# Depthwise convolution: all products from ScalarE, summed by GpSimd in SBUF instead of by TensorE in PSUM

## The chip, the cores and the metric

The kernel runs on one core of one Trainium2 chip. Its time is the device time of one execution in microseconds (us), and the figure of a version is the median of three executions. A core has five engines that work side by side, each through its own queue in a fixed order: TensorE (PE, with its weight loads as PEld), VectorE (DVE), ScalarE (ACT), GpSimd (POOL) and SyncE (SP), which issues the DMAs. An instruction that waits for a semaphore holds up everything behind it on its engine. TensorE writes to PSUM alone, the other memory on the core is SBUF.

## The reference

Two transformer-like blocks run one after the other on 256 tokens of 1024 features, in fp32. The change lies in the second block, which has three branches: attention to a memory, a convolution, and a two-way recurrence (RWKV-7) that the kernel computes with small triangular solves. Then an output projection and a layer of 16 experts follow. Shortened:

```python
def conformer_conv(pc, conv_w, conv_b, ln_g, ln_b):
    val, gate = jnp.split(pc, 2, axis=-1)
    u = val * jax.nn.sigmoid(gate)                      # 256 tokens x 384 channels
    u = lax.conv_general_dilated(u, conv_w[:, None, :], window_strides=(1,),
        padding=[(15, 15)], dimension_numbers=('NWC', 'WIO', 'NWC'),
        feature_group_count=384) + conv_b               # 31 taps, each channel by itself
    return silu(layer_norm(u, ln_g, ln_b))              # over the channels
def second_block(...):
    o_att, o_conv = memory_cross_attention(...), conformer_conv(...)
    o_rwkv = rwkv7_bidirectional(...)
    x = x + jnp.concatenate([o_att, o_conv, o_rwkv], axis=-1) @ w_out
    x = x + expert_choice_ffn(rms_norm(x), ...)         # 16 experts
```

## The kernel before

Activations lie with features on the 128 partitions and the 256 tokens along them. The 384 channels of the convolution are three tiles of 128, `u[:, 0]`, `u[:, 1]` and `u[:, 2]`, each 286 wide (256 tokens and 15 zeros on each side). A tap is one product of a shifted view `u[:, i, t:t+256]` with one number for each partition. VectorE computes tiles 0 and 1 (`conv`, L1493): one `scalar_tensor_tensor` for each tap multiplies and adds into `cacc[:, i]`, 60 of them and 2 first products. Tile 2 goes another way (`conv_pe`, L1483): ScalarE multiplies into a tile `cp`, TensorE multiplies `cp` with the unit matrix, and its 31 products add up in one PSUM bank, `pconv`, from which ScalarE writes `cacc[:, 2]`. `conv` goes on with the layer norm over the three tiles: sums over partitions by matmuls with ones (`pm`), square root, scale, SiLU, and the split into two parts (`oc`) that the output projection reads.

The convolution is woven with the recurrence. Its direction d needs, for each of three pairs of heads: `scores` (L1544: matmuls `psab`, then VectorE masks them into `LM`), `diagonal` (L1561: VectorE takes the 16x16 blocks out, tile `tm` and sums `N`; GpSimd adds the unit matrix to `LM`), and `values` (L1571: matmuls `pkt`, `prh`, `py0`, which ScalarE copies out as `bt`, `rh`, `ysum`). `blocks16` (L1608) then solves the 16x16 blocks in 15 steps: a matmul `prep`, and on VectorE a product `g` and an addition into `Gc`. `prep` needs `N` alone, so it can run ahead as far as PSUM banks are free; `g` and `Gc` are a chain. At its end VectorE spreads the blocks (`Gm`), TensorE transposes them (`pt`, L1636), and `levels` (L1645) joins blocks to 32, 64 and 128 with matmuls `pp` and `pg`. `finish` (L1684) uses the result.

What comes when is set by the generators and by the table `W` (L25): `weave` (L1751) takes one step of a main generator, and so many of the others after it. First `first_scores(0)` runs with `conv_pe`, then `other_scores(0)` and `first_scores(1)` with `blocks16(0)`, `conv_pe` and `conv`, then `levels(0)` with `blocks16(1)`, `conv` and `conv_pe`. A scheduler of the framework then puts the instructions of each engine in an order of its own, with semaphores where one needs another; that order is fixed when the kernel is built. Tiles of one tag take turns in a fixed number of buffers (`bufs`), and whoever writes a buffer again waits for its last readers. PSUM has 8 banks: five with tag `ps` (among them `pkt`, `prh`, `py0`, `prep` and half of `psab`), three with tag `pw`.

Weights of the experts (1 MB pieces, tile `ew`) are loaded into a ring of buffers that grows as tiles of the recurrence become free; SP issues them in order, and each waits until its buffer is free.

Of the kernel before, what the change touches and what calls it, by code (L numbers as in the profile page):

```python
# [11 lines left out]
F32 = mybir.dt.float32  # L12
F32R = mybir.dt.float32r
U32 = mybir.dt.uint32
AF = mybir.ActivationFunctionType
ALU = mybir.AluOpType
# [5 lines left out]
DECAY = 0.606531  # L22
MASKED = -1e30
LEAD = 5
W = 2, 2, 2, 2, 1, 0, 2, 1, 1, 8  # L25
OPB = 5, 5, 5, 5, 0
E1 = 4, 3, 2, 1
PRE = 0
# [227 lines left out]
class Body:  # L256
# [960 lines left out]
    def branches(self, x2, hi, lo, ob):  # L1217
# [53 lines left out]
        u = rb.tile([128, 3, 286], F32, name="u")  # L1271
# [188 lines left out]
        for j in range(2):  # L1460
            ps = self.pst("pvt")
# [18 lines left out]
        cw = self.v("conv_w_2").rearrange("p (k i) -> p k i", k=31)  # L1480
        cacc = rb.tile([128, 3, 256], F32, name="cacc")

        def conv_pe():  # L1483

            ps = self.pst("pconv")
            for t in range(31):
                p_ = wk2.tile([128, 256], F32, name="cp", tag="cp", bufs=2)
                self.act(p_, u[:, 2, t:t + 256], AF.Copy, scale=cw[:, t, 2:3])
                self.mm(ps[:, 0:256], self.ident, p_, t == 0, t == 30)
                yield  # L1490
            self.act(cacc[:, 2], ps[:, 0:256], AF.Identity, bias=self.v("conv_b_2", 2))

        def conv():  # L1493
            for i in range(2):
                self.ts(cacc[:, i], u[:, i, 0:256], cw[:, 0, i:i + 1], ALU.mult, self.v("conv_b_2", i), ALU.add)
                for t in range(1, 31):
                    self.stt(cacc[:, i], u[:, i, t:t + 256], cw[:, t, i:i + 1], cacc[:, i], ALU.mult, ALU.add)
                    yield
            ps = self.pst("pm")
            for i in range(3):  # L1500
                self.mm(ps[:, 0:256], self.ones, cacc[:, i], i == 0, i == 2)
            self.stt(cacc, ps[:, None, 0:256].to_broadcast([128, 3, 256]), -1.0 / 384, cacc, ALU.mult, ALU.add)
            yield
            sq = aa[0]
            self.act(sq, cacc, AF.Square)
            yield
            ps = self.pst("pm")
            for i in range(3):
                self.mm(ps[:, 0:256], self.ones, sq[:, i], i == 0, i == 2)
            rn = sq[:, 0]  # L1510
            self.act(rn, ps[:, 0:256], AF.Sqrt, scale=1.0 / 384, bias=self.eps[:, 1:2])
            nc.vector.reciprocal(rn, rn)
            yield
            self.tt(cacc, cacc, rn[:, None, :].to_broadcast([128, 3, 256]), ALU.mult)
            for i in range(3):
                self.ts(cacc[:, i], cacc[:, i], self.v("conv_ln_g_2", i), ALU.mult, self.v("conv_ln_b_2", i), ALU.add)
            yield
            s = aa[0]
            self.act(s, cacc, AF.Sigmoid)
            self.tt(cacc, cacc, s, ALU.mult)  # L1520
            yield
            ob.extend(self.kv.tile([128, 2, 256], F32R, tag=n, name="oc", bufs=1) for n in ("km", "vm"))
            ob.append(self.sq.tile([128, 2, 256], F32R, tag="sq", name="oc", bufs=2))
            for i in range(3):
                self.put_split(ob[2 + i][:, 0], ob[2 + i][:, 1], cacc[:, i])
            self.dbg("oc", cacc)
# [67 lines left out]
        def first_scores(d):  # L1594

            for i in range(3):
                scores(d, i, 0)
                yield
                diagonal(d, i)

        def other_scores(d):
            for i in range(3):
                scores(d, i, 1)
                yield
                values(d, i)
                yield
# [131 lines left out]
        def bonus():  # L1738
            for i in range(3):
                bn = wk3.tile([128, 256], F32, name="bn", tag="bn", bufs=1)  # L1740
                self.stt(bn, kds[:, i], self.v("r_k_2", i), r[:, i], ALU.mult, ALU.mult)
                ps = self.pst("pm")
                self.mm(ps[:, 0:256], self.bo, bn, True, True)
                self.tt(vv[:, i], vv[:, i], ps[:, 0:256], ALU.mult)
                self.stt(vv[:, i], vv[:, i], self.v("lnx_b_2", i), gate[:, i], ALU.add, ALU.mult)
                self.act(gate[:, i], gate[:, i], AF.Copy, scale=self.v("lnx_g_2", i))
                yield

        ct = conv()

        def weave(main, *others):  # L1751
            for _ in main:
                for g, n in others:
                    for _ in range(n):
                        next(g, 0)

        def chain(*gens):
            for g in gens:
                yield from g
        cpe, late, bon, f0 = conv_pe(), other_scores(1), bonus(), finish(0)  # L1760
        weave(first_scores(0), (cpe, W[0]))
        b0, b1 = blocks16(0), blocks16(1)
        weave(chain(other_scores(0), first_scores(1)), (b0, 2), (cpe, W[1]), (ct, W[2]))
        self.go(b0)
        weave(levels(0), (b1, 1), (ct, W[3]), (cpe, W[4]), (late, W[5]))
        self.go(b1)
        self.go(cpe)
        lv = levels(1)
        weave(itertools.islice(lv, W[9]), (ct, W[6]), (f0, 1), (late, W[7]), (bon, W[8]))
        for g in (late, bon, ct, f0):  # L1770
# [38 lines left out]
        pool, tag = late[1]  # L1809
# [382 lines left out]
```

## Time and profile before

| | us |
|---|---|
| three executions | 1173.88, 1176.94, 1177.71 (median 1176.94) |
| the profiled execution | 1175.34 |
| its span, from the first to the last instruction | 1173.5 |
| busy in the span: PE / DVE / ACT / POOL | 1062.8 / 508.2 / 417.8 / 44.4 |

The profile is one execution. Times in it count from the start of the span. A matmul in fp32 shows as two records. Lines such as L299 or L284 are those of helpers through which all matmuls or all `tensor_tensor` go, so groups are told apart by the names of the tiles: `pconv<-cp,cm` writes `pconv` and reads `cp` and `cm` (which holds the unit matrix). A busy TensorE is not one at its peak: the ends of matmuls are modelled. Recorded durations of instructions that follow each other on VectorE or ScalarE overlap by some 0.06 to 0.09 us.

### The profile page before, as it was taken

To read this page: it belongs to the slowest core of one execution; us is meant where nothing else is said; L and a number is where in the kernel's file an instruction comes from. 1 tells how busy PE (TensorE), PEld (TensorE's weight loads), DVE (VectorE), ACT (ScalarE), POOL (GpSimd) and SP (SyncE) were. 2 spreads that over 40 slices of the span, in tenths; PEclk is the share of its full clock that TensorE was granted. 3 is DMA by queue.
4 is the path that set the end of the run, shared out by engine and by line. 5 is a ranking of instruction groups with operands and counts; after the bars stand their busy time and mean duration, and the time that the engine had idled before them with its cause. 6 is when DMAs were issued, how large, how long until landed. Compare 5 with 4: busy or idle time off the path is not lost.

```text
span 1173.5 us, 19272 instructions
## 1 busy us (share of the span) xinstructions
PE 1062.8 (91%) x8188; PEld 755.2 (64%) x8188; DVE 508.2 (43%) x964; ACT 417.8 (36%) x718; POOL 44.4 (4%) x50
## 2 busy tenths in 40 slices
PE   5999999999999999999999998989978877788785
PEld 4886676899999999898679886434422222222222
DVE  3544356586555555659888546212111111111102
ACT  4542467656444444576434534101100000000003
POOL 0000000021000000101210002000000000000000
PEclk9999999999999999999799998999997888877877
DMA  9974545455655553420401378999999999999996
GB/s 354 364 278 167 179 169 208 176 182 182 209 180 181 185 190 120 166 109 1 180 1 46 144 300 337 385 419 419 420 418 420 419 419 419 419 420 419 420 419 254
DMA packets 46918, 313.88 MB, mean 267 GB/s; under 512 B 6128, under 2 KB 6896, under 8 KB 10480
## 3 DMA queue, kind: packets, MB, share of 16 engines
q1 hardware_dynamic: 46832, 312.66, 67.7%
q8 instruction: 64, 1.05, 0.4%
q14 instruction: 22, 0.18, 0.0%
HBM read 311.59 MB, written 1.05 MB: 266 GB/s over the span
## 4 chain that ended last, share of the span: by engine, by line
PE 65%; DMA 25%; DVE 4%; ACT 4%; issue 1%; POOL 1%; SPq 0%; ACTq 0%; POOLq 0%; DVEq 0%
PE pw L299 22%; PE acc L299 9%; DMA ew<-in_w_e_down_dram 9%; DMA ew<-in_w_e_up_dram 9%; DMA ew<-in_w_e_gate_dram 7%; PE pd L299 5%; PE pgu L299 4%; PE psab L299 2%; PE pada L299 2%; PE pv L299 2%; PE pqf L299 2%; PE pconv L299 1%; PE pg L299 1%; PE pp L299 1%; PE py L299 1%; PE prep L299 1%
## 5 line engine op out<-in xcount | busy, mean ns | idle before, releaser
L284 DVE TENSOR_TENSOR split<-raw,split 128x1024 fp32r<-128x1024 f32 (+2 forms) x148 | 176.8, 1203 | 114.6 <-ACT split L278 114.1
L299 PE MATMUL pgu<-ew,XE 128*32 128x256 f32 x2048 | 152.9, 435 | 48.4 <-DMA ew<-in_w_e_up_dram 41.4
L278 ACT ACTIVATE split<-raw 128x1024 fp32r<-128x1024 f32 (+2 forms) x148 | 151.8, 1032 | 124.5 <-PE pw L299 65.9
L299 PE MATMUL pd<-ew,hidT 128*32 128x512 f32 (+2 forms) x560 | 152.9, 601 | 8.3 <-DVE hidT L2086 7.8
L299 PEld LDWEIGHTS pgu<-ew,XE 128*32 128x32 f32 x2048 | 65.0, 120 | 127.8 <-DMA ew<-in_w_e_up_dram 68.3
L299 PEld LDWEIGHTS pd<-ew,hidT 128*32 128x32 f32 x560 | 41.7, 118 | 109.3 <-issue 94.6
L299 PE MATMUL acc<-uh,split 128*128 128x256 f32 x512 | 94.7, 283 | 0.0
L299 PE MATMUL pw<-h2h,split 128*128 128x256 f32 x512 | 92.9, 280 | 0.0
L296 DVE SCALAR_TENSOR_TENSOR hid<-pgu,rs,hid 128x256 f32<-128x256 f32 x16 | 7.7, 484 | 188.6 <-ACT hid L275 188.6
L296 DVE SCALAR_TENSOR_TENSOR ye<-pd,ig,ye 128x512 fp32r<-128x512 f32 (+2 forms) x35 | 24.6, 705 | 143.4 <-ACT ye L275 141.8
L275 ACT ACTIVATE hid<-pgu,rs 128x256 f32<-128x256 f32 x16 | 7.6, 473 | 214.0 <-PE pgu L299 214.0
L275 ACT ACTIVATE ye<-pd,ig 128x512 fp32r<-128x512 f32 (+2 forms) x35 | 22.8, 651 | 165.7 <-PE pd L299 165.7
L299 PEld LDWEIGHTS acc<-uh,split 128*128 128x128 f32 x512 | 80.8, 192 | 0.0
L299 PEld LDWEIGHTS pw<-h2h,split 128*128 128x128 f32 x512 | 79.3, 188 | 0.0
L299 PE MATMUL acc<-ul,split 128*128 128x256 f32 x256 | 72.5, 283 | 0.0
L299 PE MATMUL pw<-h2l,split 128*128 128x256 f32 x256 | 71.4, 279 | 0.0
L299 PE MATMUL pw<-hxh,split 128*128 128x256 f32 x320 | 61.7, 286 | 0.1
L299 PE MATMUL pw<-hmh,split 128*128 128x256 f32 x320 | 61.0, 288 | 0.0
L299 PEld LDWEIGHTS pw<-hxh,split 128*128 128x128 f32 x320 | 50.0, 188 | 9.5 <-issue 8.1
L299 PEld LDWEIGHTS pw<-hmh,split 128*128 128x128 f32 x320 | 50.5, 191 | 1.6 <-PE pz L299 0.5
L299 PEld LDWEIGHTS acc<-ul,split 128*128 128x128 f32 x256 | 49.0, 191 | 0.2 <-DVE ul L284 0.2
L299 PEld LDWEIGHTS pw<-h2l,split 128*128 128x128 f32 x256 | 48.0, 187 | 0.0
(441 smaller groups left out, 1741.6 us busy)
## 6 DMA issues: line engine op xcount, KB each, us to landing
ew<-in_w_e_gate_dram SPq DMA_DIRECT2D x64, 1024.0 KB, 19.9
ew<-in_w_e_up_dram SPq DMA_DIRECT2D x64, 1024.0 KB, 19.9
ew<-in_w_e_down_dram SPq DMA_DIRECT2D x63, 1024.0 KB, 19.9
raw<-in_w_mlp_dram SPq DMA_DIRECT2D x32, 1024.0 KB, 4.8
raw<-in_w_ada_dram SPq DMA_DIRECT2D x24, 1024.0 KB, 5.9
raw<-in_w_in_dram SPq DMA_DIRECT2D x18, 1024.0 KB, 5.0
raw<-in_w_branch_gate_dram SPq DMA_DIRECT2D x8, 1024.0 KB, 4.9
raw<-in_w_out_dram SPq DMA_DIRECT2D x4, 1024.0 KB, 6.9
```

Source lines behind the costliest of these rows:

```text
L275: self.nc.scalar.activation(out, in_, func, **kw)
L278: self.nc.scalar.activation(out, in_, AF.Copy)
L284: self.nc.vector.tensor_tensor(out=out, in0=a, in1=b, op=op)
L296: self.nc.vector.scalar_tensor_tensor(out=out, in0=a, scalar=s, in1=b, op0=op0, op1=op1)
L299: self.nc.tensor.matmul(out, lhsT, rhs, start=start, stop=stop, **kw)
```

## The change

ScalarE still computes all 31 products of tile 2, and now also the products of taps 16 to 30 of tile 1 (`TAPS = 16`). GpSimd adds them up in SBUF: those of tile 2 in `cacc[:, 2]`, those of tile 1 in a new tile `half` (named `chalf`). The first product of each is written there by ScalarE with the bias, so 30 + 14 additions remain. `pconv` and its 31 matmuls are gone. VectorE computes the 31 taps of tile 0 and 16 of tile 1, and adds `half` once. `cp` has three buffers instead of two. `conv` runs `conv_pool` to its end before it goes on. The first two numbers of `W` are now 3 and 4.

```diff
@@ -22,7 +22,8 @@
 DECAY = 0.606531
 MASKED = -1e30
 LEAD = 5
-W = 2, 2, 2, 2, 1, 0, 2, 1, 1, 8
+TAPS = 16
+W = 3, 4, 2, 2, 1, 0, 2, 1, 1, 8
 OPB = 5, 5, 5, 5, 0
 E1 = 4, 3, 2, 1
 PRE = 0
@@ -1480,22 +1481,32 @@
         cw = self.v("conv_w_2").rearrange("p (k i) -> p k i", k=31)
         cacc = rb.tile([128, 3, 256], F32, name="cacc")
 
-        def conv_pe():
-
-            ps = self.pst("pconv")
-            for t in range(31):
-                p_ = wk2.tile([128, 256], F32, name="cp", tag="cp", bufs=2)
-                self.act(p_, u[:, 2, t:t + 256], AF.Copy, scale=cw[:, t, 2:3])
-                self.mm(ps[:, 0:256], self.ident, p_, t == 0, t == 30)
-                yield
-            self.act(cacc[:, 2], ps[:, 0:256], AF.Identity, bias=self.v("conv_b_2", 2))
+        half = wk2.tile([128, 256], F32, name="chalf")
+
+        def conv_pool():
+
+            for i, ts, o in ((2, range(31), cacc[:, 2]), (1, range(TAPS, 31), half)):
+                for t in ts:
+                    x = u[:, i, t:t + 256]
+                    if t == ts[0]:
+                        self.act(o, x, AF.Identity, scale=cw[:, t, i:i + 1], bias=self.v("conv_b_2", i))
+                    else:
+                        p_ = wk2.tile([128, 256], F32, name="cp", tag="cp", bufs=3)
+                        self.act(p_, x, AF.Copy, scale=cw[:, t, i:i + 1])
+                        self.tp(o, o, p_, ALU.add)
+                    yield
 
         def conv():
-            for i in range(2):
-                self.ts(cacc[:, i], u[:, i, 0:256], cw[:, 0, i:i + 1], ALU.mult, self.v("conv_b_2", i), ALU.add)
-                for t in range(1, 31):
+            for i, n in ((0, 31), (1, TAPS)):
+                if i:
+                    self.ts(cacc[:, 1], u[:, 1, 0:256], cw[:, 0, 1:2], ALU.mult)
+                else:
+                    self.ts(cacc[:, 0], u[:, 0, 0:256], cw[:, 0, 0:1], ALU.mult, self.v("conv_b_2", 0), ALU.add)
+                for t in range(1, n):
                     self.stt(cacc[:, i], u[:, i, t:t + 256], cw[:, t, i:i + 1], cacc[:, i], ALU.mult, ALU.add)
                     yield
+            self.go(cpool)
+            self.tt(cacc[:, 1], cacc[:, 1], half, ALU.add)
             ps = self.pst("pm")
             for i in range(3):
                 self.mm(ps[:, 0:256], self.ones, cacc[:, i], i == 0, i == 2)
@@ -1746,6 +1757,7 @@
                 self.act(gate[:, i], gate[:, i], AF.Copy, scale=self.v("lnx_g_2", i))
                 yield
 
+        cpool = conv_pool()
         ct = conv()
 
         def weave(main, *others):
@@ -1757,14 +1769,13 @@
         def chain(*gens):
             for g in gens:
                 yield from g
-        cpe, late, bon, f0 = conv_pe(), other_scores(1), bonus(), finish(0)
-        weave(first_scores(0), (cpe, W[0]))
+        late, bon, f0 = other_scores(1), bonus(), finish(0)
+        weave(first_scores(0), (cpool, W[0]))
         b0, b1 = blocks16(0), blocks16(1)
-        weave(chain(other_scores(0), first_scores(1)), (b0, 2), (cpe, W[1]), (ct, W[2]))
+        weave(chain(other_scores(0), first_scores(1)), (b0, 2), (cpool, W[1]), (ct, W[2]))
         self.go(b0)
-        weave(levels(0), (b1, 1), (ct, W[3]), (cpe, W[4]), (late, W[5]))
+        weave(levels(0), (b1, 1), (ct, W[3]), (cpool, W[4]), (late, W[5]))
         self.go(b1)
-        self.go(cpe)
         lv = levels(1)
         weave(itertools.islice(lv, W[9]), (ct, W[6]), (f0, 1), (late, W[7]), (bon, W[8]))
         for g in (late, bon, ct, f0):
```

The orders below are those of the built programs, one row for instructions that follow each other and read alike. First ScalarE, before: from the first product `cp` of tile 2 to the first copies (`bt`, `rh`, `ysum`) of `values` in direction 0.

```order
L275 ACTIVATE cp<-u,vec 128x256 x2
L278 ACTIVATE om<-pom 128x256
L275 ACTIVATE vv<-pad_4841,mu_4820 128x256 x2
L275 ACTIVATE cp<-u,vec 128x256 x2
L278 ACTIVATE vtok<-pvt 128x384 x2
L275 ACTIVATE cp<-u,vec 128x256 x13
L278 ACTIVATE bt_5760<-pkt 128x256
L278 ACTIVATE rh_5761<-prh 128x256
L278 ACTIVATE ysum<-py_5870 128x256
L275 ACTIVATE cp<-u,vec 128x256
```

The same stretch of ScalarE after the change:

```order
L276 ACTIVATE cp<-u,vec 128x256 x3
L279 ACTIVATE om<-pom 128x256
L276 ACTIVATE vv<-pad_4841,mu_4820 128x256 x2
L276 ACTIVATE cp<-u,vec 128x256 x6
L276 ACTIVATE chalf<-u,vec 128x256
L276 ACTIVATE cp<-u,vec 128x256 x3
L279 ACTIVATE vtok<-pvt 128x384 x2
L276 ACTIVATE cp<-u,vec 128x256 x29
L279 ACTIVATE bt_5761<-pkt 128x256
L276 ACTIVATE cp<-u,vec 128x256
L279 ACTIVATE rh_5762<-prh 128x256
L276 ACTIVATE cp<-u,vec 128x256
```

Before, 17 of 31 products stand ahead of the first `bt`; now 41 of 44 do, and the two first products (`chalf` here, `cacc` much earlier) as well. Every product from the fourth on waits until GpSimd is through with the third one before it, since `cp` has three buffers.

GpSimd before, from the last work of the projections to the first `diagonal`:

```order
L287 TENSOR_TENSOR ex_5047<-pr,ex_5047 128x3x256
L287 TENSOR_TENSOR ex_5048<-pr,ex_5048 128x3x256
L1443 COPY kds<-LM_5581 128x768
L287 TENSOR_TENSOR LM_5663<-LM_5663,pr 128x768
L1445 TENSOR_TENSOR kds<-kds,LM_5663 128x768
L1568 TENSOR_TENSOR LM_5767<-LM_5767,cm 128x512
```

GpSimd after, from its first addition of the convolution on:

```order
L288 TENSOR_TENSOR cacc<-cacc,cp 128x256
L1444 COPY kds<-LM_5581 128x768
L288 TENSOR_TENSOR cacc<-cacc,cp 128x256 x5
L288 TENSOR_TENSOR LM_5663<-LM_5663,pr 128x768
L288 TENSOR_TENSOR cacc<-cacc,cp 128x256
L1446 TENSOR_TENSOR kds<-kds,LM_5663 128x768
L288 TENSOR_TENSOR cacc<-cacc,cp 128x256 x14
L1579 TENSOR_TENSOR LM_5768<-LM_5768,cm 128x512
L288 TENSOR_TENSOR cacc<-cacc,cp 128x256 x7
L1579 TENSOR_TENSOR LM_5769<-LM_5769,cm 128x512
L288 TENSOR_TENSOR cacc<-cacc,cp 128x256 x2
L288 TENSOR_TENSOR chalf<-chalf,cp 128x256 x4
```

After the last of these rows come `LM_5770`, then the ten other additions into `chalf`, then the three `diagonal` additions of direction 1. So 34 additions stand ahead of the third `LM`, and 38 ahead of what the 41st product needs.

TensorE before, around the first `values` (with the semaphores that are waited for):

```order
L299 MATMUL pconv<-cp,cm 128x256 [waits Activation_49] x2
L299 MATMUL psab<-ex_5047 128x256
L299 MATMUL pconv<-cp,cm 128x256 [waits Activation_49]
L299 MATMUL prep<-N,sel 128x192 [waits DMAHW3_49,DVE_49]
L299 MATMUL prep<-N,sel 128x192 [waits PE_49]
L303 MATMUL pkt<-cm,aa_5045 128x128 [waits PE_49]
L303 MATMUL pkt<-cm,ex_5047 128x128
L299 MATMUL prh<-vtok,LM_5835 128x64 [waits PE_49]
L299 MATMUL prh<-vtok,LM_5835 128x64 x3
L299 MATMUL py_5870<-LM_5835,vtok 64x128 [waits DVE_49]
L299 MATMUL py_5870<-LM_5835,vtok 64x128 x3
L299 MATMUL prep<-N,sel 128x192 [waits Activation_49] x2
```

TensorE after, in the same place:

```order
L300 MATMUL prep<-N,sel 128x192 [waits DMAHW3_49,DVE_49]
L300 MATMUL prep<-N,sel 128x192
L304 MATMUL pkt<-cm,aa_5045 128x128
L304 MATMUL pkt<-cm,ex_5047 128x128
L300 MATMUL prh<-vtok,LM_5842 128x64 x4
L300 MATMUL py_5883<-LM_5842,vtok 64x128 x4
L300 MATMUL prep<-N,sel 128x192 [waits DVE_49]
L300 MATMUL prep<-N,sel 128x192 [waits Activation_49]
L300 MATMUL psab<-ex_5047 128x256 [waits Activation_49]
L300 MATMUL psab<-ex_5047 128x256
```

`pkt` is followed by `prh`, `py`, and the third and fourth `prep`; the fourth waits for ScalarE, and it gets the bank for which the copy `bt` has to be done, the `psab` behind it that of `rh`. In both versions the third or the fourth `prep` waits for ScalarE; what stands ahead of `bt` there is what moved.

## Rows read from the trace of the kernel before

**Rows 1.** which engine is busy, clock and DMA, in four stretches

```profile
core 0: us, PE busy (x) PEld busy (x) DVE busy (x) ACT busy (x) POOL busy (x), PEclk, DMA share, GB/s
554.00:558.00 4.00, 1.58 (x13) 1.20 (x12) 4.00 (x9) 0.50 (x2) 0.15 (x1) 1.00 0.00 0
558.00:571.00 13.00, 13.00 (x35) 8.64 (x36) 12.36 (x16) 3.38 (x9) 4.57 (x3) 0.51 0.97 382
...
584.00:610.30 26.30, 25.80 (x145) 18.66 (x143) 22.84 (x64) 10.03 (x23) 2.81 (x2) 1.00 0.00 1
```

**Rows 2.** the chain of waits (start us, us, what), 580 to 660

```profile
610.35 1.31 PE pt L303 x12
...
619.12 0.43 PE pconv L299 x2
...
641.94 1.30 PE pm L299 x6
...
647.45 1.30 PE pm L299 x6
```

**Rows 3.** timeline of ScalarE (start us, us, what, [idle before <-releaser])

```profile
558.04 0.91 ACT L275 ACTIVATE cp<-u,vec 128x256 f32<-128x256 f32 x2
...
584.71 0.38 ACT L278 ACTIVATE bt<-pkt 128x256 f32<-128x256 f32 x1 [0.30 <-PE pkt L303]
585.55 0.38 ACT L278 ACTIVATE rh<-prh 128x256 f32<-128x256 f32 x1 [0.46 <-PE prh L299]
```

**Rows 4.** groups of GpSimd instructions (xcount | busy us, mean ns | idle)

```profile
L1568 POOL TENSOR_TENSOR LM<-LM,cm 128x512 f32<-128x512 f32 x6 | 8.0, 1338 | 37.8 <-DVE tm L284 34.8 <-ACT cp L275 1.5 <-PE psab L299 1.4
L287 POOL TENSOR_TENSOR sa<-sa,sq 128x256 f32<-128x256 f32 x8 | 6.2, 778 | 10.1 <-ACT sq L275 9.8
...
L287 POOL TENSOR_TENSOR LM<-LM,pr 128x768 f32<-128x768 f32 x1 | 1.9, 1885 | 3.1 <-DVE LM L293 3.1
L1445 POOL TENSOR_TENSOR kds<-kds,LM 128x768 f32<-128x768 f32 x1 | 1.9, 1863 | 0.1
...
L1443 POOL COPY kds<-LM 128x768 f32<-128x768 f32 x1 | 0.8, 823 | 4.6 <-DVE LM L284 4.6
```

**Rows 5.** timeline of GpSimd, 550 to 606

```profile
550.44 3.71 POOL L287 TENSOR_TENSOR ex<-pr,ex 128x768 f32<-128x768 f32 x2 [75.96 <-DVE stm L291]
...
562.65 1.89 POOL L287 TENSOR_TENSOR LM<-LM,pr 128x768 f32<-128x768 f32 x1 [3.08 <-DVE LM L293]
...
604.97 1.55 POOL L1568 TENSOR_TENSOR LM<-LM,cm 128x512 f32<-128x512 f32 x1 [1.96 <-DVE tm L284]
```

**Rows 6.** timeline of VectorE in the same places

```profile
551.21 3.42 DVE L293 TENSOR_SCALAR LM<-aa,vec,oneka 128x256 f32<-128x256 f32 x3
...
562.39 2.42 DVE L296 SCALAR_TENSOR_TENSOR vv<-pad,vec,vv 128x256 f32<-128x256 f32 x2
...
604.91 0.48 DVE L296 SCALAR_TENSOR_TENSOR cacc<-u,vec,cacc 128x256 f32<-128x256 f32 x1
```

**Rows 7.** a group of VectorE instructions, 556.8 to 570.3

```profile
L284 DVE TENSOR_TENSOR aa<-aa,ex 128x768 f32<-128x768 f32 x2 | 1.9, 946 | 0.0
```

**Rows 8.** groups of VectorE instructions, 589.2 to 610.3

```profile
L296 DVE SCALAR_TENSOR_TENSOR cacc<-u,vec,cacc 128x256 f32<-128x256 f32 x12 | 5.7, 474 | 0.0
L284 DVE TENSOR_TENSOR LM<-psab,cr 128x512 f32<-128x512 f32 x8 | 5.5, 687 | 2.6 <-PE psab L299 2.0 <-PE py L299 0.5
...
L284 DVE TENSOR_TENSOR tm<-LM,cr 128x512 f32<-128x512 f32 x3 | 2.1, 684 | 0.0
L1566 DVE TENSOR_REDUCE N<-tm 128x64 f32<-128x512 f32 x2 | 2.0, 1015 | 0.0
```

**Rows 9.** timeline of VectorE, the fourth step of the first block solve

```profile
589.28 0.30 DVE L284 TENSOR_TENSOR g<-prep,Gc 128x144 f32<-128x144 f32 x1
```

**Rows 10.** windows of 2 us at the start of the expert stage

```profile
732.00:734.00 2.00, 2.00 (x23) 1.24 (x23) 0.25 (x2) 0.47 (x1) 0.00 (x0) 0.93 0.02 4
...
736.00:738.00 2.00, 2.00 (x25) 1.21 (x24) 0.48 (x1) 0.47 (x1) 0.00 (x0) 1.00 1.04 426
```

## The prediction

> **What bounds the kernel now.** I read the windows by stage first, then the chain of waits, then the queues of the engines that touch the convolution. In the stretch that the change rewrites (558 to about 634 us) TensorE and VectorE are both nearly full and GpSimd is nearly free: from 584 to 610.3 TensorE has records for 25.8 of 26.3 us, VectorE 22.8, GpSimd 2.8 [rows 1]. That invites the change. But the reader should look at what the stretch has to reach: the transposes `pt`, which open `levels(0)` at 610.35 [rows 2]. They need the end of the first block solve, whose chain `g`, `Gc` runs on VectorE, and that needs `prep` from TensorE, which stops as soon as the copies `bt` and `rh` on ScalarE are late, since they free its banks. Before, `bt` starts at 584.71, 0.30 after ScalarE went idle: it waits for TensorE and nothing else [rows 3]. So ScalarE's queue is not the bound now, and the question is whether it becomes one.
>
> After the stretch the delay has nowhere to go. At 732 to 734 the DMAs stand almost still (share 0.02) and from 736 they are full [rows 10]: at 732 the ring of expert weights holds all it can, and from there the DMAs follow the rate at which TensorE frees buffers. A stretch that ends x later moves all that by x.
>
> **What goes.** 31 matmuls with the unit matrix. The two late ones stand in the chain in `levels(0)`, 0.43 each [rows 2]: 0.9 us less. The other 29 lie before `pt`, where they are filling between waits; what their room is worth is in the block solve below. VectorE loses 14 steps of tile 1 and gains one addition.
>
> **What comes: 44 additions on GpSimd.** The trace has the same operation in the same shape, `sa<-sa,sq`, each waiting for the one before: 0.778 us mean [rows 4]. ScalarE needs 0.46 for a product (two in 0.91, [rows 3]), so GpSimd sets the pace and ScalarE, three buffers ahead, waits in its queue. ScalarE's order decides: 41 products stand ahead of the first `bt`, and the 41st waits for the 38th addition. GpSimd's queue up to there: 38 x 0.778 = 29.6; three `diagonal` additions of 1.338 = 4.0; the product and sum for `kds`, 1.885 + 1.863; its copy 0.823 [rows 4]. Together 38.2. The first `cp` is ready at 558.5, half of the pair at 558.04 [rows 3], so the 38th addition ends at 596.7 if nothing disturbs GpSimd.
>
> It will be disturbed. At 550.44 two GpSimd products run for 3.71, and three VectorE instructions that start at 551.21 take 3.42 instead of about 0.4 each; at 562.39 two take 2.42 instead of 0.9 beside the GpSimd product at 562.65; the other way round, the addition at 604.97 takes 1.55 against a mean of 1.338, having started 0.06 after a VectorE one of 0.48 [rows 4 to 6]. So the two take turns when both read SBUF. What a turn costs GpSimd I take as VectorE's duration less a part of each GpSimd instruction that does not grow with size: 256 more elements cost 1.338 - 0.778 = 0.56, so 0.778 - 0.56 = 0.22. The VectorE instructions in the stretch whose operands are both in SBUF, by its order, which does not change there, and one turn each: five of 768 elements at 0.946 [rows 7], twelve of 256 at 0.474 and three `tm` at 0.684 [rows 8]. That makes 5 x 0.73 + 12 x 0.25 + 3 x 0.46 = 8.0. The 38th addition ends at 604.7, the 41st product at 605.2, and `bt` starts there: 20.5 us later than the 584.71 of before. Bounds: no turns at all, 597.2; whole durations (4.7 + 5.7 + 2.1 = 12.5), 609.7.
>
> [...]
>
> **The block solve after `bt`.** When TensorE stops at the fourth `prep`, VectorE has done three steps and stands before the `g` of the fourth. Before, that `g` starts at 589.28 [rows 9] and `pt` at 610.35 [rows 2]: 21.1 us. After, it can start some 0.9 after `bt` (0.38 for the copy, one `prep`, the hand-overs), at 606.1. What VectorE has to do from there: by the order two steps of the convolution and one masking `LM` fewer (0.474 x 2 + 0.687), one `tm` and one sum `N` more (0.684 + 1.015) [rows 8]: even. So `pt` at 606.1 + 21.1 = 627.2, 16.8 later than before. Bounds: 2.6 of the 21.1 are waits for `psab` and `py` [rows 8], part of them behind `pconv`, and may go: 18 us. On the other side six additions and three of 1.338 are left to GpSimd and take turns with VectorE: 27 us.
>
> **The rest.** `conv` can go on only when GpSimd is through, some 10 us after `bt`, well before `pt`; its matmuls `pm` stand later in TensorE's order, so no wait is added there. Six of them (1.30 + 1.30, [rows 2]) move from `levels(1)` into `levels(0)`: zero, with bounds -3 and +4 for what ScalarE's table loads and the copies queued behind them do in the new place. VectorE's relief in `levels(0)` I count at nothing, because TensorE has the longer list there.
>
> TensorE's clock: 4 us with little work (1.58 busy, 554 to 558) were followed by 13 us at 0.51, the lower of its two levels [rows 1]. After the change TensorE waits some 20 us for `bt`, so it will come back at the lower level. Most of that lies beside VectorE's 21 us; I take +1, bounds 0 and 6.4 (half of those 13).
>
> **Sum** against the profiled execution: 16.8 - 0.9 + 1.0 = 16.9, so 1175.3 + 16.9 = 1192.2. Its time lies 1.6 under the median of the runs, so the forecast for a median is 1193. The bounds together give 1175.3 + 1 to 1175.3 + 36.
>
> **The rivals.**
>
> *The lock is as strict as it can be* (chance 0.16): every VectorE instruction costs GpSimd its whole length, and in the block solve VectorE in turn waits for whole additions. `bt` at 609.7, the solve 25 us: `pt` at 635.6, 25 later, 1200 to 1202. For it: the 2.42 and 3.42 [rows 6]. Against: the 3.71 [rows 5].
>
> *The late copies are hidden* (chance 0.08): `bt` at 597.2, the solve in 18 us, thus `pt` at 616.1, 5.8 later; with the 0.9 and 3 us won in `levels(1)` about 2 us remain, 1177 to 1179, no change that can be told. For it: the waits in [rows 8] and an emptier TensorE. Against: VectorE is busy nearly all through that stretch [rows 1].
>
> *It pays* (chance 0.04): TensorE's stretch shrinks by the `pconv` matmuls and nothing waits for `bt`. It would need 38 additions and the other 8.6 us of GpSimd within the 26.2 us from 558.5 to 584.7, so 0.46 us for an addition; from there on the products on ScalarE set the pace and the gain is the 0.9 and the 2.6 of waits, 1172. Against it: 0.778, eight times measured [rows 4].
>
> The forecast itself has 0.72. Its own range is 1186 to 1200.
>
> **How the numbers follow.** A measurement of this kernel tells apart changes of over 0.3%, 3.5 us. Faster by more needs "it pays" in full: 0.03. Within 0.3%: nearly all of "hidden" and the rest of "it pays", 0.08. Slower: 0.89. The range for 8 in 10 takes in the strict lock up to 1207 and, below, a `bt` halfway to its lower bound: 1183.
>
> **What would show it.** In the changed profile: GpSimd additions `cacc<-cacc,cp` back to back from 558.5, starts 0.8 to 1.1 apart; ScalarE's waits on GpSimd at its products, 10 us or more in all; the first `bt` near 605; TensorE idle or at the lower clock in the 20 us before; `pt` near 627; the ring's pause at the start of the expert stage some 17 later than 732. It is wrong if `bt` comes before 595, if the fourth `prep` doesn't wait for it, or if the stretch from `pt` to the end of `levels(1)` is shorter than before by more than 3 us.

## The result, and the profile after

The changed kernel takes 1206.72 us (median of four, 1202.7 to 1207.59), before it was 1176.95 on the same chip. The ratio is 1.0264, with a 95% interval of 1.0245 to 1.0284, so it is some 30 us slower, 31 by the ratio. The forecast was 1193, and the ratio times the 1176.94 of before lies at 1208, just over the upper end of the range. The profiled execution took 1207.59, 32.25 more than that of before. It begins 1.4 us late, long before the change (GpSimd's `ex` at 551.81 against 550.44 in [rows 5]); this is not counted below.

The windows of the same stretch, columns as in [rows 1]:

```profile
558.00:571.00 13.00, 12.57 (x37) 8.23 (x37) 12.41 (x15) 6.96 (x16) 10.70 (x10) 0.57 0.86 338
571.00:584.00 13.00, 8.79 (x25) 6.01 (x24) 13.00 (x17) 6.35 (x13) 12.14 (x13) 0.50 0.17 68
584.00:605.00 21.00, 8.54 (x30) 6.29 (x30) 8.03 (x14) 11.34 (x24) 19.59 (x26) 0.50 0.00 0
605.00:636.00 31.00, 30.53 (x87) 19.64 (x86) 14.27 (x38) 3.45 (x9) 5.24 (x6) 0.50 0.00 1
...
645.00:660.00 15.00, 15.00 (x127) 14.98 (x126) 12.62 (x38) 4.86 (x10) 0.00 (x0) 0.99 0.00 1
```

The rows from 571 and from 584 are what the prediction described: GpSimd is nearly full, and TensorE works 8.54 of the 21 us up to 605. The row from 605 to 636 is the one that it didn't have: TensorE has records for 30.53 of 31 us at clock 0.50, the lower of its two levels, and VectorE, which was to be the chain there, is busy for 14.27. Only from 645 on the clock is at the upper level again (0.99). Before, the 26 us of the same work ran at 1.00 [rows 1].

ScalarE (columns as in [rows 3]), and its group of products from 558 to 606 (xcount | busy us, mean ns | idle before, by releaser):

```profile
559.40 1.30 ACT L276 ACTIVATE cp<-u,vec 128x256 f32<-128x256 f32 x3
...
603.26 0.51 ACT L276 ACTIVATE cp<-u,vec 128x256 f32<-128x256 f32 x1 [0.29 <-POOL chalf L288]
603.68 0.36 ACT L279 ACTIVATE bt<-pkt 128x256 f32<-128x256 f32 x1
...
642.94 0.60 ACT L279 ACTIVATE Tm<-pt 128x512 f32<-128x512 f32 x1 [16.59 <-PE pt L304]
```

```profile
L276 ACT ACTIVATE cp<-u,vec 128x256 f32<-128x256 f32 x44 | 22.1, 508 | 20.9 <-POOL cacc L288 17.4 <-POOL chalf L288 3.3
```

`bt` starts at 603.68, at once behind a product that waited for GpSimd, and the products together waited 20.7 us for GpSimd's additions. Then GpSimd:

```profile
559.99 0.73 POOL L288 TENSOR_TENSOR cacc<-cacc,cp 128x256 f32<-128x256 f32 x1 [4.48 <-ACT cp L276]
...
571.73 14.17 POOL L288 TENSOR_TENSOR cacc<-cacc,cp 128x256 f32<-128x256 f32 x14
...
595.79 3.13 POOL L288 TENSOR_TENSOR chalf<-chalf,cp 128x256 f32<-128x256 f32 x4
...
600.10 7.94 POOL L288 TENSOR_TENSOR chalf<-chalf,cp 128x256 f32<-128x256 f32 x10
```

With VectorE at work 14 additions take 14.17 us, 1.01 each; while VectorE stands still (from 593.5 to 607), four take 3.13 and ten 7.94, 0.78 to 0.79 each, the 0.778 of [rows 4]. TensorE, in the same columns:

```profile
575.53 2.07 PE L300 MATMUL psab<-ex,aa 64*128 64x256 f32 x4 [3.46 <-ACT vtok L279]
...
590.99 1.01 PE L300 MATMUL prep<-N,sel 128*128 128x192 f32 x2
604.10 1.01 PE L300 MATMUL prep<-N,sel 128*128 128x192 f32 x2 [12.09 <-ACT bt L279]
...
641.79 2.82 PE L304 MATMUL pt<-cm,Gm 128*128 128x128 f32 x12 [0.24 <-DVE Gm L285]
```

The fourth `prep` waits 12.09 us for `bt`, as foreseen. Earlier, `psab` waits 3.46 us for `vtok`, a copy that also stands in ScalarE's queue behind 12 products; the prediction had missed it. `pt` starts at 641.79, 31.4 later than in [rows 2], and VectorE waits for TensorE where it had a chain to work on:

```profile
570.02 2.56 DVE L285 TENSOR_TENSOR aa<-aa,ex 128x768 f32<-128x768 f32 x1
...
607.14 0.69 DVE L285 TENSOR_TENSOR LM<-psab,cr 128x512 f32<-128x512 f32 x1 [13.68 <-PE psab L300]
...
629.54 0.69 DVE L285 TENSOR_TENSOR LM<-psab,cr 128x512 f32<-128x512 f32 x1 [4.93 <-PE psab L300]
```

The first of these rows shows the turns on VectorE's side too: the instruction of 0.946 in [rows 7] takes 2.56 beside GpSimd's `kds` and additions (before, GpSimd was idle there). At the start of the expert stage the pause of the ring lies at 764 (before at 732, [rows 10]), so what `pt` lost went to the end undiminished:

```profile
764.00:766.00 2.00, 2.00 (x23) 1.21 (x21) 0.45 (x1) 0.47 (x1) 0.00 (x0) 0.83 0.03 12
...
768.00:770.00 2.00, 2.00 (x28) 1.35 (x24) 0.48 (x1) 0.47 (x1) 0.00 (x0) 1.00 0.93 393
```

### The profile page after: what moved, and what is told of

Its sections match the earlier page's. It is cut to its first block, busy times and chain, and to the rows that moved or that the text cites. A ratio compares the mean times of both kernels' runs of the same rounds, so it can differ in the third digit from the quotient of the medians.

```text
span 1205.6 us, 19219 instructions
## 1 busy us (share of the span) xinstructions
PE 1073.1 (89%) x8126; PEld 763.1 (63%) x8126; DVE 510.2 (42%) x950; ACT 425.7 (35%) x732; POOL 81.1 (7%) x94
## 4 chain that ended last, share of the span: by engine, by line
PE 61%; DMA 26%; DVE 4%; ACT 4%; POOL 3%; issue 2%; SPq 0%; ACTq 0%; POOLq 0%; DVEq 0%
PE pw L300 21%; DMA ew<-in_w_e_up_dram 10%; PE acc L300 9%; DMA ew<-in_w_e_down_dram 8%; DMA ew<-in_w_e_gate_dram 7%; PE pd L300 4%; PE pgu L300 4%; PE pada L300 2%; POOL cacc L288 2%; PE pv L300 2%; PE pqf L300 2%; PE psab L300 2%; PE prep L300 1%; PE pg L300 1%; PE pp L300 1%
```

## The experiments

Theory A is that of the prediction, extended: `bt` comes late, TensorE stops for it, and the stop leaves TensorE at the lower clock. Theory B: the 31 products with the unit matrix had kept TensorE's clock up, and without them the block solve runs at the lower level whether `bt` is late or not. Theory C: GpSimd's additions cost the most, through their turns with VectorE, or the order of the solve does.

Times are medians of 4 to 12 executions. Ratios are to runs of before on the same chip; before took 1172 to 1177 on the chips used, so a time is held against another row's, or a forecast, by the ratio. `bt` (its first copy on ScalarE) and `pt` (its first matmul) are from the one profiled execution and count from its start; by the `ex` of [rows 5], the stretch begins 1.2 us earlier (e8) to 2.5 us later (e3) than before.

| | what | ratio [95%] | us | `bt` | `pt` | from `bt` to `pt` | clock between |
|---|---|---|---|---|---|---|---|
| before | | 1 | 1176.9 | 584.7 | 610.2 | 25.5 | 1.00 |
| after | the change | 1.0264 [1.0245, 1.0284] | 1206.7 | 603.7 | 641.8 | 38.1 | 0.50 |
| e1 | 12 products ahead of `bt` | 1.0171 [1.0148, 1.0194] | 1194.8 | 587.3 | 628.4 | 41.1 | 0.50 |
| e2 | 20 idle products before `bt` | 1.0269 [1.0243, 1.0294] | 1206.3 | 603.2 | 640.3 | 37.1 | 0.50 |
| e3 | short additions | 1.0138 [1.0111, 1.0166] | 1191.1 | 588.9 | 627.0 | 38.1 | 0.50 |
| e4 | tile 2 alone | 1.0167 [1.0138, 1.0196] | 1194.2 | 591.9 | 630.0 | 38.1 | 0.50 |
| e5 | before, short unit products | 1.0253 [1.0228, 1.0279] | 1204.2 | 596.0 | 639.3 | 43.3 | 0.50 |
| e6 | e1 with 46 idle products | 1.0154 [1.0130, 1.0177] | 1194.0 | 592.5 | 627.0 | 34.5 | mostly 1.00 |
| e7 | after with 46 idle products | 1.0245 [1.0223, 1.0267] | 1204.5 | 606.9 | 636.0 | 29.1 | 1.00 from 612 |
| e8 | before, 12 early idle products | 1.0001 [0.9984, 1.0018] | 1174.3 | 579.8 | 604.1 | 24.3 | 1.00 |
| e9 | e6 with short additions | 1.0058 [1.0037, 1.0079] | 1181.7 | 586.3 | 614.6 | 28.4 | 1.00 |
| e10 | tile 1's 15 taps on TensorE | 1.0047 [1.0028, 1.0065] | 1181.3 | 586.5 | 612.3 | 25.8 | 1.00 |
| e11 | e10 with early idle products | 1.0103 [1.0080, 1.0126] | 1187.1 | 585.2 | 614.8 | 29.5 | 1.00 |
| e12 | e2 with 28 idle products | 1.0258 [1.0229, 1.0288] | 1202.6 | 603.8 | 631.1 | 27.3 | see below |
| e13 | e3 with early idle products | 1.0066 [1.0029, 1.0104], two groups, below | 1178.2 | 589.2 | 614.8 | 25.6 | 1.00 to 610 |
| e14 | e1 with early idle products | 1.0100 [1.0070, 1.0130] | 1187.2 | 587.5 | 628.6 | 41.1 | 0.50 |

In every row, the profiled execution ends 563 to 572 us after `pt` (before 565, after the change 566). So most of the time is decided at `pt`, as the prediction had it, and what remains to be explained is `bt` and the way from `bt` to `pt`. The exceptions are e6, e7, e10 and e11, which lose another 3 to 7 us behind `pt`.

**e1, the order of ScalarE.** `in_turn` is a helper of the kernel: what is traced inside is queued behind the instruction traced before it on that engine.

```diff
-                        self.act(p_, x, AF.Copy, scale=cw[:, t, i:i + 1])
+                        with self.in_turn("Activation"):
+                            self.act(p_, x, AF.Copy, scale=cw[:, t, i:i + 1])
                         self.tp(o, o, p_, ALU.add)
```

> The changed kernel, but ScalarE issues each product behind what was traced before it, so 12 products stand ahead of the first bt instead of 41; the number of products and additions is the same. Theory A (the queue of ScalarE, and the low clock it leaves TensorE in): bt near 587, TensorE back at the upper clock by about 595, pt near 613 to 618, 1178 to 1186 us. Theory B (the products with the unit matrix were what brought TensorE's clock back): bt near 587 as well, but the clock stays at 0.50 until the transposes, pt near 623 to 630, 1189 to 1196. Theory C (the 44 additions themselves, through their turns with VectorE): 1195 or more.

`bt` came at 587.33, waiting for TensorE and not for ScalarE. Yet the clock stayed down for another 40 us, by the windows of e1:

```profile
584.00:596.00 12.00, 12.00 (x40) 8.54 (x38) 6.52 (x17) 4.88 (x11) 4.68 (x6) 0.50 0.00 1
...
608.00:620.00 12.00, 12.00 (x39) 8.40 (x39) 8.69 (x23) 5.90 (x13) 8.39 (x12) 0.50 0.01 1
...
632.00:644.00 12.00, 12.00 (x103) 11.98 (x102) 11.33 (x30) 5.39 (x11) 3.90 (x5) 1.00 0.01 1
```

That refutes theory A as the whole cause. The time, 1194.8 (1197 by the ratio), lies at the upper end of B's range and the lower end of C's and doesn't tell the two apart; the clock does speak for B.

**e2, idle products before `bt`.**

```diff
+                if d == 0 and kk == 2:
+                    for _ in range(20):
+                        with self.in_turn("PE"):
+                            self.mm(ps[:, 256:512], self.ident, u[:, 2, 0:256], True, True)
```

> The changed kernel with 20 idle products of 128x256 (unit matrix by a tile of u, result not used) on TensorE behind the third prep, where it waited 12.1 us for bt. bt stays near 603.7. Theory A: TensorE comes back at the upper clock, the stretch from bt to pt shrinks from 38.1 us to 22 to 27, 1190 to 1196. Theory C and any reason that lies in the order of the block solve: the stretch stays at 35 to 40, 1204 to 1212.

The windows of e2 around `bt` (603.2) and behind it:

```profile
596.00:600.00 4.00, 4.00 (x20) 3.54 (x19) 4.00 (x5) 1.53 (x3) 3.84 (x5) 1.00 0.00 0
...
604.00:608.00 4.00, 4.00 (x10) 2.31 (x8) 4.00 (x5) 1.69 (x5) 3.61 (x5) 0.50 0.00 0
...
612.00:636.00 24.00, 23.20 (x71) 14.98 (x70) 10.72 (x31) 1.92 (x5) 2.52 (x2) 0.50 0.00 1
```

The idle products did bring the clock up (0.81 from 592 to 596, then 1.00 and 0.97 up to 604), but it was down again one window later (0.50) and stayed there: 37.1 us from `bt` to `pt`, and no time won. It doesn't tell why, since 20 products ended 2.9 us before `bt`, and that gap could have dropped the clock; e12 closes it.

**e3, short additions.** `self.tp(o[:, 0:16], o[:, 0:16], p_[:, 0:16], ALU.add)` in place of the full width; 240 of the 256 columns are not summed.

> The changed kernel, but each addition on GpSimd takes 16 of the 256 columns (the others are left out), so GpSimd is no longer the pace. Theory A: ScalarE runs its products at about 0.42 to 0.46 each, bt at 585 to 588, TensorE never stops for long, pt near 611 to 615, 1173 to 1180. Theory B: bt as early, but the clock stays low for want of the products with the unit matrix, 1186 or more.

The windows of e3 behind its `bt`:

```profile
596.00:608.00 12.00, 11.69 (x36) 7.56 (x35) 5.43 (x16) 1.16 (x4) 0.00 (x0) 0.50 0.00 0
608.00:620.00 12.00, 11.84 (x35) 7.97 (x36) 5.91 (x18) 0.88 (x3) 1.27 (x1) 0.50 0.01 1
```

`bt` came at 588.94, GpSimd has nothing to do from 596 to 608, and the way from `bt` to `pt` is 38.1 us, to the tenth what it is after the change. So those 38 us have nothing to do with GpSimd or with the wait for `bt`: they are the solve at the lower clock (0.50). From e3 to the changed kernel `bt` is 14.7 later, `pt` 14.8, the time 15.6 (14.8 by the ratios): with the clock down, a late `bt` costs one for one.

**e4, one tile.** `TAPS = 31`, without `half`; the second tile stays on VectorE.

> Half of the change: the 31 products of the third tile go to GpSimd, the second tile stays whole on VectorE. 30 products stand ahead of bt, the last of them waits for the 27th addition. Theory A: bt near 592, TensorE waits 1 to 4 us for it instead of 12.1; if the clock comes back soon after, 1183 to 1190, if it stays low as long as with the whole change, 1192 to 1198. Theory C: in proportion to the additions, 30 of 44 of the loss, 1197.

`bt` at 591.85 as expected, again 38.1 to `pt`, 1194.2: the row in which the clock "stays low as long as with the whole change" (1192 to 1198). Theory C's 1197 fits as well: 30 of 44 of 2.64% is 1.80%, within the interval of 1.38 to 1.96%. So the time of e4 doesn't decide between them; the unchanged 38.1 at clock 0.50, with fewer additions, speaks against C.

**e5, the kernel before with narrow unit products.**

```diff
-                self.mm(ps[:, 0:256], self.ident, p_, t == 0, t == 30)
+                n = 256 if t in (0, 30) else 16
+                self.mm(ps[:, 0:n], self.ident, p_[:, 0:n], t == 0, t == 30)
```

> The kernel before with one thing less: 29 of its 31 products with the unit matrix take 16 of the 256 columns (the other columns of the third tile's sum are left out). GpSimd does no addition, ScalarE the same 31 products. Theory B (these products hold TensorE's clock up in the block solve): bt at 585 to 589 as before, but TensorE at 0.50 from 560 to the transposes, pt at 622 to 630, 1187 to 1194 us. Theory A (only a late bt costs): 1172 to 1178.

The windows of e5 before, within and near the end of the solve:

```profile
560.00:572.00 12.00, 12.00 (x33) 8.30 (x32) 10.99 (x15) 2.61 (x6) 3.75 (x2) 0.50 0.92 384
...
596.00:608.00 12.00, 12.00 (x38) 7.66 (x37) 5.12 (x14) 1.91 (x5) 0.00 (x0) 0.50 0.00 0
...
620.00:632.00 12.00, 12.00 (x42) 9.06 (x40) 4.89 (x14) 2.81 (x7) 1.26 (x1) 0.50 0.00 0
```

This speaks for B: no addition on GpSimd, no work added anywhere, and TensorE is at 0.50 from 560 to past 640. The 1204.2 is more than expected: a 16-column product at the lower clock still takes TensorE 0.25 per record, and the order had moved a little (23 products ahead of `bt` instead of 17), so `bt` waited for TensorE until 596.

**e6 and e7, idle products in place of those taken out.** One more line behind each product, in a bank of their own that nobody reads; e6 on e1, e7 on the changed kernel:

```diff
+                    with self.in_turn("PE"):
+                        self.mm(idle[:, 0:256], self.ident, x, True, True)
```

> The kernel of the first experiment (12 products ahead of bt) with 46 idle products of 128x256 on TensorE, one behind each product's place in the text, so that TensorE has as many columns to do as with the unit matrix before; no engine waits for them. Theory B: the clock is back at the upper level by about 575 to 585, the stretch from bt to pt is 21 to 27 us instead of 41, 1174 to 1184. If the additions on GpSimd were what made that stretch long: 1192 to 1200.

> The changed kernel itself (41 products ahead of bt) with the same 46 idle products on TensorE. bt stays late, 600 to 604. Theory B with the queue of ScalarE as a second cost of its own: the clock comes back soon after bt, pt 22 to 28 us behind it, 1190 to 1197. If the low clock came from the wait for bt alone: as the changed kernel, 1204 to 1210.

In both the clock came back: in e6 from 0.50 (568 to 580) to 1.00 (584 to 588), with 0.57 from 588 to 592 and from 612 to 616 and 1.00 for the rest up to `pt`. In e7 it was up from 576 on (1.00), but for a stretch near 588 (0.64 from 588 to 592), fell while TensorE waited for the late `bt` (0.72 from 596 to 600, then 0.50), and came back right behind it:

```profile
600.00:604.00 4.00, 0.00 (x0) 0.00 (x0) 0.00 (x0) 1.81 (x4) 3.77 (x5) 0.50 0.00 0
...
608.00:612.00 4.00, 4.00 (x12) 2.90 (x11) 1.39 (x4) 0.00 (x0) 0.78 (x2) 0.57 0.00 0
612.00:616.00 4.00, 4.00 (x25) 3.38 (x24) 3.27 (x10) 0.38 (x1) 0.00 (x0) 1.00 0.02 4
```

Its way to `pt` shrank from 38.1 to 29.1. But the times hardly fell. In e7 (1204.5) `bt` came 3.2 later: the stretch begins 0.7 later, and in the order that was built all 44 products stand ahead of `bt` instead of 41, at GpSimd's 0.8 us each; another 2.8 us are lost behind `pt`, where idle products go on. In e6 `bt` came 5.2 later, the way was 6.6 shorter, and 4.5 us more than in e1 went behind `pt`. In e6 VectorE now sets the pace, busy for 40.5 of the 44 us from 584 to 628. Groups of VectorE's instructions from `bt` to `pt` (xcount | busy us, mean ns), first those of e6:

```profile
L297 DVE SCALAR_TENSOR_TENSOR cacc<-u,vec,cacc 128x256 f32<-128x256 f32 x21 | 14.2, 685 | 0.0
L285 DVE TENSOR_TENSOR Gc<-Gc,g 128x156 f32<-128x156 f32 (+12 forms) x13 | 8.4, 643 | 0.1
```

and those of e9, the next experiment:

```profile
L297 DVE SCALAR_TENSOR_TENSOR cacc<-u,vec,cacc 128x256 f32<-128x256 f32 x21 | 9.9, 481 | 0.0
...
L285 DVE TENSOR_TENSOR Gc<-Gc,g 128x156 f32<-128x156 f32 (+12 forms) x13 | 3.6, 275 | 0.1
```

**e9** is e6 with the short additions of e3.

> The kernel of e6 (12 products ahead of bt, 46 idle products on TensorE) with additions of 16 of the 256 columns (the rest is left out). If GpSimd's turns with VectorE are the third cost, which shows once the clock is up and bt is on time: VectorE's taps in the solve at 0.47 instead of 0.8 to 1.0, pt at 606 to 614 instead of 627, 1171 to 1181 us. If the idle products or the order of the solve are what is left: pt at 620 or later, 1187 to 1195.

A tap takes 685 ns on average beside full additions and 481 without (474 in [rows 8]), an addition `Gc` 643 and 275; `pt` moves from 627.0 to 614.6 and the time from 1194.0 to 1181.7. So full additions are a third cost, 12 us, which shows only when the clock is up and `bt` on time: theory C was right in its mechanism, and hidden in e1 behind the lower clock. Of the 12.3 us at `pt`, 6.1 are the way from `bt` to `pt`; there the turns are shown, since the taps and `Gc` alone take VectorE 9.1 us more. The other 6.2 lie ahead of `bt`: 1.7 are a later start of e6's profile, and the clock was lower there too (0.50 from 568 to 580, 0.57 from 588 to 592), so how much of them is turns is not shown. What remains in e9 (0.58%) is the 46 idle products and the short additions themselves; it wasn't split further.

**e8, e10, e11, the other way: more on TensorE.** e8 puts four idle products behind each of the first three `scores` of the kernel before. e10 sums taps 16 to 30 of tile 1 by the unit matrix as well, in columns 256 to 512 of `pconv`. e11 is both.

> The kernel before with 12 idle products of 128x256 on TensorE between the first scores, where it has 13 us at the lower clock. Theory B: the clock comes back some us before the 571 of before; VectorE is busy in that stretch, so the gain is 0 to 3 us, 1171 to 1177. If idle products only cost their time: 1177 to 1182.

> The opposite of the change: taps 16 to 30 of the second tile go to ScalarE as in the changed kernel, but TensorE sums them with the unit matrix, in the free half of the bank that sums the third tile; GpSimd gets nothing. VectorE has 14 steps less, TensorE 15 products more. If VectorE bounds the two solves once TensorE's clock is up: 4 to 7 us less, 1169 to 1173. If TensorE bounds them: 15 x 0.43 = 6 more, 1178 to 1183.

> The kernel of e10 with the 12 idle products of e8 between the first scores, so that TensorE's clock does not fall at 559. If the clock before 571 counts once VectorE has less to do: 1 to 5 us below e10. If not: 0 to 4 above it.

e8 has the clock at 1.00 all the way to `pt`, and `pt` 6 us earlier in its profile (4.9 net of the start; it is the fastest of the ten executions), yet its ten runs (1171.4 to 1179.5) can't be told from before. e10 and e11 are slower. The time of e10 is the one expected for solves that TensorE bounds, but only 2.1 of the 7.0 us by which its profile is longer lie before `pt`, and the way from `bt` to `pt` is 25.8 as against 25.5; e11 lost more than the 0 to 4 expected on top. Where the rest of both goes, behind `pt`, was not tested. No version here beats the kernel before.

**e12, no gap before `bt`.** As e2 with 28.

> The kernel of e2 with 28 idle products instead of 20: e2 left TensorE 2.9 us without work right before bt, and its clock fell there. With 28 there is no such gap. If that gap is why the clock fell: it stays at the upper level after bt, the stretch from bt to pt is 22 to 28 us, 1190 to 1196. If the block solve's own matmuls do not hold the clock up (theory B): it falls to 0.50 within some us after bt although TensorE goes on without a gap, the stretch stays at 33 to 38, 1202 to 1208.

TensorE in e12:

```profile
591.58 13.99 PE L301 MATMUL prep<-u,cm 128*128 128x256 f32 x56
605.40 0.49 PE L301 MATMUL prep<-N,sel 128*128 128x192 f32 x2
...
612.74 0.48 PE L305 MATMUL pkt<-cm,aa 128*128 128x128 f32 x1 [4.94 <-DVE g L286]
```

VectorE, and the windows:

```profile
593.96 14.89 DVE L298 SCALAR_TENSOR_TENSOR cacc<-u,vec,cacc 128x256 f32<-128x256 f32 x17
```

```profile
604.00:608.00 4.00, 3.80 (x18) 2.71 (x16) 4.00 (x6) 2.24 (x6) 3.61 (x6) 1.00 0.02 4
...
612.00:616.00 4.00, 3.26 (x11) 2.29 (x12) 3.29 (x10) 0.38 (x1) 0.00 (x0) 0.52 0.00 0
616.00:620.00 4.00, 4.00 (x19) 2.82 (x18) 1.50 (x4) 0.77 (x2) 0.00 (x0) 0.63 0.00 0
620.00:632.00 12.00, 8.90 (x57) 6.45 (x57) 10.07 (x26) 1.33 (x4) 2.53 (x2) 1.00 0.00 0
```

The median is what B expected, the way from `bt` to `pt` what the other did, and neither saw what happened. With no gap the clock stayed up past `bt` (1.00 to 612). Then TensorE stopped for 4.94 us, because VectorE's queue (its order changed with the 28 products) had 17 taps in a row and more ahead of `g`, and the clock fell (0.52 from 612 to 616). And it came back near 619, with the solve's own matmuls alone, and held (1.00 from 620 to 632). So "the solve can't hold the clock" is too strong. The profiled execution was the fastest of five (1197.9; the others 1202.0 to 1204.9), and the one with the highest granted clock on average over the execution (0.936; the others 0.924 to 0.929).

**e13 and e14: where are the products needed?** The early idle products of e8, on e3 and on e1.

> The kernel of e3 (additions of 16 columns, the rest left out: bt on time, no turns with VectorE, and there the clock stayed at 0.50 from 560 to 628) with 12 idle products on TensorE between the first scores, and none later. If the products with the unit matrix are needed only to bring the clock back (or to keep it from falling at 559), and the block solve then holds it: 1.00 until the transposes, pt 20 to 26 us behind bt, 1172 to 1180. If they are needed all through: the clock falls to 0.50 again within the solve, pt 32 to 38 us behind bt, 1185 to 1192.

> The changed kernel in whole, with the order of e1 (12 products ahead of bt) and 12 idle products between the first scores, none later; all additions on GpSimd in full. If the clock comes back at the first scores and the solve holds it: as e6, where VectorE's turns with GpSimd are what is left, 1187 to 1194. If the solve does not hold it: as e1, 1193 to 1198.

The ten runs of e13 fall in two groups, six at 1176.6 to 1178.2 and four at 1188.2 to 1190.4; those of e14 spread from 1180.6 to 1193.9. The profiled execution of e13 took 1178.2, that of e14 1193.4. The windows of e13:

```profile
576.00:580.00 4.00, 4.00 (x9) 2.33 (x9) 1.11 (x2) 3.40 (x9) 2.94 (x9) 0.50 0.00 0
...
584.00:588.00 4.00, 3.66 (x19) 2.70 (x17) 3.92 (x8) 1.95 (x6) 2.44 (x6) 1.00 0.00 0
...
592.00:604.00 12.00, 11.53 (x68) 7.89 (x67) 8.49 (x26) 2.30 (x6) 0.00 (x0) 1.00 0.01 2
```

And of e14:

```profile
576.00:580.00 4.00, 4.00 (x18) 2.99 (x19) 4.00 (x8) 0.00 (x0) 2.51 (x3) 1.00 0.00 0
...
584.00:588.00 4.00, 3.05 (x14) 2.60 (x15) 4.00 (x10) 0.38 (x1) 1.27 (x1) 0.82 0.00 0
...
592.00:604.00 12.00, 12.00 (x37) 7.56 (x37) 5.05 (x12) 4.88 (x11) 5.97 (x9) 0.50 0.01 2
```

In e13 the clock came back and the solve held it (1.00 from 584 to 608) until it ran out of work near 610 (0.73 from 608 to 612, with TensorE busy for 0.45 of 4 us); in e14 it had come back too (1.00 from 576 to 584), and fell near 587 (0.82, then 0.50), in a window in which TensorE worked for 3.05 of 4 us. So without the unit products the solve ran at either level: at the upper in e13 and at the end of e12, at the lower in the changed kernel, e1 to e4 and e14. With them in full it held in all four profiles (before, e8, e10, e11); with idle products in their place it held in e7 from 612 and in e9, and fell for a stretch near 612 in e6 (0.57), behind a wait of TensorE for VectorE (2.1 us). Only one execution of each kernel has a profile, but each has its granted clock on average over the execution: 0.940 to 0.946 in the six faster ones of e13, 0.925 to 0.932 in the four others. If there are only the two levels, that is some 34 us more at the lower one, about the length of the stretch from 582 to 615 (an estimate from these averages). So one program goes either way from execution to execution, 12 us apart. With the clock up, the six faster executions of e13 lie only 0.2% above before (median 1177.5 to 1175.1). In e14 the three slowest (1193.4 to 1193.9) have the lowest averages as well, 0.922 to 0.930, the others 0.934 to 0.944; between its 1181 and its 1187 the averages don't tell.

## Why the prediction was wrong

Its direction held, and so did the chain up to `bt`:

- *Additions 0.8 to 1.1 apart, back to back:* 0.78 alone, 1.01 beside VectorE.
- *ScalarE waits 10 us or more:* 20.7.
- *`bt` near 605.2:* 603.7, or 602.3 without the late start. The turns were put at 8.0 us up to the 38th addition. It ended near 603.2, 43.2 after the first began, 5.0 over the 38.2 of work. With whole VectorE durations, the upper bound, it would have been 12.5; the trace shows the turns and not that price on GpSimd's side. That every VectorE instruction with both operands in SBUF costs a turn, as the 8.0 counts them, no run shows: beside GpSimd three taps took 0.95 to 0.97 (0.47 in [rows 8]) and one `aa` 2.56, but the three `tm` 0.70 each (0.68), hardly more than before, and the masking `LM`, which reads PSUM, 0.68 (0.69).
- *The fourth `prep` waits for `bt`:* 12.09 us. *The ring moves as a whole:* its pause went from 732 to 764, as far as `pt` moved.
- *The terms behind `pt`* (-0.9 and 0): the profiled execution ends 565.8 behind `pt`, before 565.2, so +0.6, and the 0.9 did not come.

The step that failed is the block solve with the clock. It says that `pt` comes 21.1 us behind the fourth `g`, 22.0 behind `bt`, as before, that TensorE "will come back at the lower level", and that "most of that lies beside VectorE's 21 us; I take +1, bounds 0 and 6.4". Measured: 38.1, so 16.1 too short, or 15.1 with the 1 us allowed for the clock. That is the miss: the profile is 32.25 longer instead of 16.9, and the other terms (`bt` 2.9 earlier than forecast, net of the start, the start 1.4 later, 1.5 more behind `pt`) cancel out by luck. Two things were wrong in it. The solve was taken for VectorE's chain, because VectorE was busy 22.84 of 26.3 us; but TensorE had 25.8 in the same row [rows 1], and at half the clock it is TensorE's by far (30.53 of 31 us, VectorE 14.27). And the bound 6.4 took the 13 us at the lower level of before for the longest such stretch. But it was `pconv`, from 568 on (2.07 us from 568.14, 1.52 from 570.86, with `pvt` between), that filled TensorE when the clock rose near 572 (0.50 up to 571.5, 1.00 from 572); the change takes away just these products, and after it the stretch at the lower level is 85 us long (560 to 645). The question "what else do the removed matmuls do" was answered with their time (0.9 us) and never with their effect on the clock.

Two numbers do not follow from the terms given for them: 1192.2 and 1.6 make 1193.8 and not 1193, and a `bt` halfway to its lower bound is 4 us earlier, which gives 1190 and not the 1183 of the range. The measured time lies outside the range all the same.

The rival "strict lock", by which every VectorE instruction costs GpSimd its whole length, had the time nearly right (1200 to 1202) for a wrong reason: `bt` was not at 609.7, and from 608 to 631, in the middle of the long solve, GpSimd did nothing.

How the 30 us divide, by the runs: with short additions (e3) 1.38% of the 2.64% are left, so 1.26%, or 15 us, go with the late `bt`. The other 1.38%, 16 us, go with the missing unit products; 12 of them are the clock in the solve, by the two groups of e13. The full additions' third cost, 12 us from e9 to e6, is in neither: it lies under the lower clock, and appears where that is cured. The costs are not to be added up.

## What to carry to other kernels

Before matmuls are taken from TensorE, look in the windows at what its clock does while they run, and price the stretch behind them at both levels: filler that costs nothing may be what keeps the clock up (here 1.00 from `bt` to `pt` with the unit products in full, 0.50 with narrow ones in e5). Curing one cost can only show the next one, so an experiment that cures one and wins nothing has not cleared it (e6 and e9). And count what a helper on another engine puts ahead of the copies in an in-order queue: 41 products at GpSimd's pace ahead of one 0.4 us copy cost half of the loss here.

## What the runs showed of the hardware that was not expected

- TensorE with records for 30.53 of 31 us (605 to 636, matmuls of 64 rows or of 64 to 192 columns among them) stayed at a granted clock of 0.50; the clock was at 0.99 again from 645 on, where the 128x128 transposes `pt` (from 641.8) and products `pp` (from 644.4) run. The trace shows two levels: of windows of 0.25 us over the whole span, 4662 of 4692 before and 4789 of 4820 after read 0.50 or 1.00. But a TensorE that was busy by its records did not bring the upper one here; why, no run here shows.
- Executions of one program on one core can lie 12 us apart in two groups (e13, medians 1177.5 and 1189.9), and their average granted clocks lie apart too (0.940 to 0.946 and 0.925 to 0.932).
- The turns between VectorE and GpSimd cost both: an addition of 128x256 on GpSimd 0.78 or 1.01, a tap on VectorE 0.48 or 0.69 on average (e9 and e6), and a single instruction of 768 elements 2.56 instead of 0.95.
